# Attention scores and a filter product over 128 rows instead of 64, by zero padding, in a two-layer hybrid encoder

## The chip, the core and the metric

The kernel runs on one core of a Trainium2 chip. Such a core has a matrix engine (TensorE, PE in the profile; its weight loads are listed apart as PEld), two engines for elementwise work (VectorE, DVE; ScalarE, ACT), a slower general one (GpSimd, POOL), and SyncE (SP), which here only issues DMA transfers. Each engine works through its own instructions in program order, and semaphores hold one back until what it needs from another has been done.

The metric is device time of one execution in microseconds (us), smaller is better. Three executions of the kernel before took 1847.16, 1850.46 and 1852.89 us; the median is 1850.46 us.

## The reference

Two groups of tokens, a sample of 512 and a prompt of 256, go through the same two layers of width 1024. Each layer is a token mixer and a convolutional feed-forward network, with a norm ahead of and behind each. Layer 0 mixes with a gated MLP, layer 1 with two long convolutions whose filters a small MLP makes; beside the mixer, in both layers, runs cross-attention with 4 heads of 64 channels into 256 memory tokens of each group. Cut to what the change touches:

```python
def memory_cross_attention(q, mem, mem_g, w_kv):
    q = q.reshape(bsz, length, 4, 64)
    kv = (rms_norm(mem, mem_g) @ w_kv).reshape(bsz, 256, 2, 4, 64)
    k, v = kv[:, :, 0], kv[:, :, 1]
    s = jnp.einsum('bshd,bmhd->bhsm', q, k) * 64 ** -0.5     # the scores: 64 channels are summed
    p = jax.nn.softmax(s, axis=-1)
    return jnp.einsum('bhsm,bmhd->bshd', p, v).reshape(bsz, length, 256)

def hyena_filters(length, w1, b1, w2, b2, w3, freq):
    h = jnp.sin(fr * (feat @ w1 + b1))
    h = jnp.sin(fr * (h @ w2 + b2))                          # (length, 64)
    h = (h @ w3).reshape(length, 2, 2, 768)                  # 64 hidden units are summed
    return h * decay[:, None, None, :]

# per layer
att = memory_cross_attention(q, mem, ...)
x = x + rms_norm(concatenate([mix, att]) @ w_out)
x = x + rms_norm(conv_ffn(rms_norm(x)))
```

## The kernel before, in words

**Precision.** A float32 product is made of three matmuls in the type fp32r: each operand is split into a high part and the rest, and `mm3` (L497 to 501) adds high·high, high·low and low·high in one PSUM bank. The split is a pair of instructions, a copy to fp32r on ACT and a subtraction on DVE (`split`). So each weight tile that arrives by DMA (`wr`, 128x1024) becomes two tiles `ws`, and nearly all PE work is matmuls with 128 rows of weights and 256, 384 or 512 columns.

**Stages.** Layer 0: `pre` (norm and transposes), `kv0` (memory keys and values), the mixer, attention (`att0`), projection `out0`, then the feed-forward network (`up0`, `down0`). Layer 1 the same with `kv1`, `rows` and `conv` (short convolutions, and the long ones as matrix DFTs, tiles `dft` and `iv`), `att1`, `out1`, `up1`, `down1`. The filters for layer 1 are made during layer 0. In the profile the products of the feed-forward network and other projections are called `rp`, `fmp`, `fmb`, `fma`, `bQ`, `bP`, `bA`; `tps` are PE transposes through the tile `ident`.

**Keys.** `kv` (L819 to 866) makes, per layer, one tile `kT` [128, 2, 2, 512]: two heads on the upper and lower 64 partitions, then high and low part, head pair, and memory token. It is split from PSUM in 2 pieces of 128x512 per layer. The weights wk and wv go to buffers of their own (`own` true, tag `wkv`) or into the ring of ten `ws` buffers.

**Scores.** `attention` (L876 to 926) goes over 2 head pairs and 3 pairs of token tiles. For each, two PSUM banks `sc0`, `sc1` take the scores of the two heads: 2 token tiles × 3 products × 2 heads, the heads innermost, and each matmul uses the 64 partitions of its head (`r`) in both operands. That is 72 matmuls of 64 rows and 256 columns per layer. Behind them come the maximum (`mx`) on DVE, the exponentials (`e`) on ACT, transposes (`eps`) and `pv`.

**Filters.** `filters` (L1083 to 1163) makes `h` = `h2s`·`w3h` in 36 pairs: a matmul over 128 rows (the upper 64 the high part of the hidden units, the lower 64 their rest, against the high part of w3, which stands on both halves), and one over 64 rows for the low part of w3.

**Order of the work.** The program is recorded first. `Order` (L92 to 364) notes each operation with what it depends on, then `schedule` runs a list scheduler with its own costs (`cost`, L194 to 215): at each step the engine that can start earliest takes, among its ready operations, the one with the lowest rank, which is its number in the program plus a number from the table `BIAS` by stage and kind (L190: `pe`, `ve`, `dma`, `load`). None may be more than `AHEAD` operations beyond the oldest one not yet placed. All are emitted in that order from L364, so nearly every row of the profile has this line, and operations are told apart by tile names. Buffers come from small pools: 14 tiles of 8 KB per partition (`s8`), 27 of 4 KB (`s4`, of which 10 may be `ws`, 4 `wr`), and 8 PSUM banks.

Of the kernel before, what the change touches and what calls it, by code (L numbers as in the profile page):

```python
# [13 lines left out]
F32 = mybir.dt.float32  # L14
F32R = mybir.dt.float32r
I32 = mybir.dt.int32
AF = mybir.ActivationFunctionType
ALU = mybir.AluOpType
# [18 lines left out]
SEVEN = (1,)  # L37


AHEAD = 526  # L40
BIAS = {
    ('', 'dma'): -394,
    ('att0', 'pe'): -540, ('att0', 've'): -40,
    ('att1', 'pe'): -20, ('att1', 've'): -1151,
    ('block0', 'pe'): 175, ('block0', 've'): -278,
    ('block1', 'load'): 474, ('block1', 'pe'): -79, ('block1', 've'): -165,
    ('block2', 'load'): -843, ('block2', 'pe'): 33, ('block2', 've'): -155,
    ('conv', 'dma'): 395, ('conv', 'pe'): -273, ('conv', 've'): 32,
    ('down0', 'load'): -240, ('down0', 'pe'): -17,
    ('down0h0', 've'): -268,  # L50
    ('down0h1', 'dma'): -91, ('down0h1', 've'): 142,
    ('down1', 'load'): 163,
    ('down1h1', 'dma'): -343,
    ('filters', 'dma'): -120, ('filters', 'pe'): 253, ('filters', 've'): 275,
    ('gate', 'dma'): -215, ('gate', 've'): 147,
    ('kv0', 'dma'): -178, ('kv0', 'load'): -188, ('kv0', 'pe'): -894, ('kv0', 've'): -120,
    ('kv1', 'dma'): 162, ('kv1', 'load'): -202, ('kv1', 'pe'): -293, ('kv1', 've'): -427,
    ('mixed', 'pe'): -395, ('mixed', 've'): -1071,
    ('normv', 've'): -69,
    ('out0', 'load'): 518, ('out0', 'pe'): -124,  # L60
    ('out0h0', 've'): 79,
    ('out0h1', 'dma'): 302, ('out0h1', 'pe'): 31, ('out0h1', 've'): 102,
    ('out1', 'load'): -67, ('out1', 'pe'): -7,
    ('out1h0', 've'): 42,
    ('out1h1', 'dma'): -23, ('out1h1', 'pe'): 103, ('out1h1', 've'): -16,
    ('pre', 'dma'): -836, ('pre', 'load'): -835, ('pre', 'pe'): -114, ('pre', 've'): 48,
    ('presplit', 'dma'): -7, ('presplit', 've'): 464,
    ('q0', 'load'): -164, ('q0', 'pe'): 313, ('q0', 've'): 363,
    ('q1', 'load'): -618, ('q1', 've'): -315,
    ('rows', 'load'): -344, ('rows', 'pe'): 302, ('rows', 've'): -40,  # L70
    ('up0', 'load'): -444, ('up0', 'pe'): 22, ('up0', 've'): -873,
    ('up1', 'pe'): 59, ('up1', 've'): 343,
    ('x2', 'load'): 8, ('x2', 'pe'): 1,
}
LN_EPS = 1e-5
ATT_SCALE = 0.125
# [15 lines left out]
class Order:  # L92
# [100 lines left out]
    @staticmethod  # L193
    def cost(eng, method, kw, args, outs, ins):  # L194
        n = max(int(np.prod([c for s, c in x.ap[1:]])) for x in outs)
        psum = any(x.space == bass.MemoryType.PSUM for x in ins)
        if eng == "tensor":
            if method == "transpose":
                return 110
            if kw["rhs"].dtype == F32R:  # L200
                return 13.5 + n / 2.4 if n >= 256 else 229
            return 20 + 4 * n / 2.4
        if eng == "scalar":
            c = (52 if psum else 95) + 0.833 * n
            return c + (190 if isinstance(kw.get("bias"), bass.AP) or isinstance(kw.get("scale"), bass.AP) else 0) + \
                (90 if "accum_out" in kw else 0)
        if eng == "vector":
            if method in ("tensor_scalar", "tensor_copy") and not psum:
                return 68 + 0.522 * n
            if method == "tensor_reduce" or method == "bn_stats":  # L210
                n = max(int(np.prod([c for s, c in x.ap[1:]])) for x in ins)
            return (130 if method == "scalar_tensor_tensor" else 69) + 1.042 * n
        if eng == "gpsimd":
            return 180 + 2.105 * n
        return 450


# [209 lines left out]
class Prog:  # L427
# [391 lines left out]
    def kv(self, l, out, own):  # L819
        nc, a = self.nc, self.a  # L820
        g = self.gain(a["norm_mem"][l], name="gmem")
        kT = self.s8([128, 2, 2, 512], F32R, "kT")
        vS = self.s8([128, 2, 4, 256], F32R, "vS")
        out += [kT, vS]
        wk = wv = None
        for grp in range(2):
            mT = [self.s8([128, 8, 256], F32R, f"mT{h}") for h in range(2)]
            for i in range(2):
                m = self.t4(name="mem")
                nc.sync.dma_start(out=m, in_=a["mem"][2 * grp + i])  # L830
                mn = self.t4(name="mn")
                ss = self.small([128, 1], "mss")
                nc.scalar.activation(mn, m, AF.Square, accum_out=ss)
                r = self.rstd_of(ss, D, EPS, "mr")
                nc.vector.scalar_tensor_tensor(out=mn, in0=m, scalar=r, in1=g, op0=ALU.mult, op1=ALU.mult)
                s = slice(i * 128, (i + 1) * 128)
                for b in range(2):
                    ps = self.bank("mps")
                    for j in range(4):
                        k = 4 * b + j  # L840
                        nc.tensor.transpose(ps[:, j * 128:(j + 1) * 128], mn[:, k * 128:(k + 1) * 128], self.ident)
                    self.split(mT[0][:, 4 * b:4 * b + 4, s], mT[1][:, 4 * b:4 * b + 4, s],
                               ps.rearrange("p (k t) -> p k t", k=4))
                yield
            wk = wk or [self.wload(a["wk"][l, j], own) for j in range(2)]
            ps = self.bank("kps")
            for j in range(2):
                o = ps[:, j * 256:(j + 1) * 256]
                for k in range(KD):
                    ks = slice(k * 128, (k + 1) * 128)  # L850
                    self.mm3(o, wk[j][0][:, ks], wk[j][1][:, ks], mT[0][:, k], mT[1][:, k], k == 0, k == KD - 1)
            gs = slice(grp * 256, (grp + 1) * 256)
            self.split(kT[:, 0, :, gs], kT[:, 1, :, gs], ps.rearrange("p (j m) -> p j m", j=2))
            yield
            wv = wv or [self.wload(a["wv"][l, c], own) for c in range(2)]
            ps = self.bank("vps")
            for i in range(2):
                o = ps[:, i * 256:(i + 1) * 256]
                s = slice(i * 128, (i + 1) * 128)
                for k in range(KD):  # L860
                    w = wv[k // 4]
                    ks = slice((k % 4) * 256, (k % 4 + 1) * 256)
                    self.mm3(o, mT[0][:, k, s], mT[1][:, k, s], w[0][:, ks], w[1][:, ks], k == 0, k == KD - 1)
            self.split(vS[:, 0, 2 * grp:2 * grp + 2], vS[:, 1, 2 * grp:2 * grp + 2],
                       ps.rearrange("p (i m) -> p i m", i=2))
            yield
# [9 lines left out]
    def attention(self, q, kT, vS, put, hps=range(2)):  # L876
        nc = self.nc
        qS, qP = q
        for hp in hps:
            pS = [self.s8([128, 2, 2, NS], F32R, f"pS{h}") for h in range(2)]  # L880
            pP = [self.s4([128, 2, 2, NP], F32R, f"pP{h}") for h in range(2)]
            for ip in range(TT // 2):
                m0 = 0 if ip < 2 else 256
                qt, pt, o = (qS, pS, ip * 256) if ip < 2 else (qP, pP, 0)
                scs = [self.bank(f"sc{h}") for h in range(2)]
                for i in range(2):
                    t0 = o + i * 128
                    for n, (p, q) in enumerate(((0, 0), (0, 1), (1, 0))):
                        for h in range(2):
                            r = slice(h * 64, h * 64 + 64)  # L890
                            nc.tensor.matmul(scs[h][:, i * 256:(i + 1) * 256], lhsT=qt[r, p, hp, t0:t0 + 128],
                                             rhs=kT[r, q, hp, m0:m0 + 256], start=n == 0, stop=n == 2)
                for h in range(2):
                    sc = scs[h]
                    mx = self.small([128, 2], "mx")
# [187 lines left out]
    def filters(self):  # L1083
# [35 lines left out]
        for th in range(3):  # L1119
            for o in range(2):  # L1120
# [3 lines left out]
                self.tt(w3[:, 512:768], w3[:, 0:256], w3[:, 256:512], ALU.add)  # L1124
                self.tt(w3[:, 768:], w3[:, 0:256], w3[:, 256:512], ALU.subtract)
                wh = self.t4(shape=[128, 2, 512], dt=F32R, name="w3h")
                self.split(wh[:, 0], wh[:, 1], w3[:, 512:])
                hfS = [self.s8([128, 4, 2, 256], F32R, f"hfS{p}") for p in range(2)]
                hfP = [self.s4([128, 2, 2, 256], F32R, f"hfP{p}") for p in range(2)]
                for tp in range(3):  # L1130
# [5 lines left out]
                    for i in range(2):  # L1136
                        t = 2 * tp + i
                        ps = self.bank("h3")
                        s = slice(t * 128, (t + 1) * 128)
                        nc.tensor.matmul(ps, lhsT=hs[:, s], rhs=wh[:, 0], start=True, stop=False)  # L1140
                        nc.tensor.matmul(ps, lhsT=hs[:64, s], rhs=wh[:64, 1], start=False, stop=True)
                        for d in range(2):
                            self.tt(hf[:, i, d], ps[:, d * 256:(d + 1) * 256], dec[:, i * 256:(i + 1) * 256], ALU.mult)
                    if tp != 1:
# [71 lines left out]
    def mixer_b(self, hT, kvo):  # L1216
# [80 lines left out]
                            x2[j][:, t0:t0 + n].rearrange("p (i r) -> p r i", r=nr), ALU.mult)  # L1297
                    self.split(get(0, 2 * th + j), get(1, 2 * th + j), om[:, t0:t0 + n])

        kv = self.kv(1, kvo, True)  # L1300
        with nc.of("rows"):
            v = rows_of(0, 0)
        nc.run(kv, "kv1")
# [153 lines left out]
```

## Time and profile before

| | |
|---|---|
| median of 3 runs | 1850.46 us (1847.16 to 1852.89) |
| profiled execution, device time | 1850.47 us |
| its span in the trace | 1848.3 us |
| PE | 1802.5 us busy, 98% of the span, 9504 matmuls |
| DVE | 1142.6 us, 62% |
| ACT | 698.1 us, 38% |
| POOL | 73.3 us, 4% |
| mean granted clock of PE | 0.98 |

A row of the profile names the line, the engine, the operation, what it writes and reads (`out<-in`), the shape, and how often (x). For a matmul the first pair is rows × columns of the weights that it was loaded with, so `64*128` is a contraction over 64 partitions; the second is the moving operand. Matmul records overlap: each shows the time from its issue to its modelled end, and matmuls are pipelined, so what one costs is read from one start to the next, not from its length. In brackets behind a row stands how long the engine was idle before it, and what ended that. The slices of the page are 46.2 us wide; PEclk is the clock granted to PE in tenths.

### The profile page before, as it was taken

The page shows a single profiled execution, that of the slowest core. Times are in us where ns is not written, and L with a number is a line of the kernel's source. Part 1 is how long each engine was busy: PE and PEld are TensorE (multiplying, and loading weights), DVE is VectorE, ACT ScalarE, POOL GpSimd, SP SyncE. Part 2 cuts the span into 40 slices and gives each one's busy share as a digit, 9 for nine tenths or more (in the row PEclk, how much of TensorE's full clock was granted, in tenths as well). Part 3 has the DMA queues.
Part 4 walks back from the last instruction along what each step waited for, and adds up shares of the span by engine and source line. Part 5 has one row for each costly group of instructions (what it writes and reads, how often), then busy time and mean ns, then how long its engine had stood idle before and what let it go on. Part 6 is the DMA issues. An engine that isn't in the chain of part 4 may idle for free.

```text
span 1848.3 us, 23739 instructions
## 1 busy us (share of the span) xinstructions
PE 1802.5 (98%) x9504; PEld 1553.9 (84%) x9504; DVE 1142.6 (62%) x1671; ACT 698.1 (38%) x1073; POOL 73.3 (4%) x155
## 2 busy tenths in 40 slices
PE   8999999999999999999999999989699999999998
PEld 6978878788888888888898887868599999998886
DVE  6354465646455557553857894763888787874352
ACT  6363334323323326443521224142544344443330
POOL 1000020000000000000300000000300000000001
PEclk9999999999999999999999998979899999999999
DMA  6212162232233134588844232212322323356522
GB/s 259 81 40 80 35 211 84 65 110 78 79 115 103 59 124 163 201 295 301 316 159 160 82 95 98 69 56 70 126 86 86 114 87 103 103 201 249 189 79 102
DMA packets 66829, 236.18 MB, mean 128 GB/s; under 512 B 7475, under 2 KB 7679, under 8 KB 64160
## 3 DMA queue, kind: packets, MB, share of 16 engines
q1 hardware_dynamic: 66720, 234.68, 36.6%
q8 instruction: 75, 1.23, 0.3%
q14 instruction: 34, 0.28, 0.1%
HBM read 183.00 MB, written 51.64 MB: 127 GB/s over the span
## 4 chain that ended last, share of the span: by engine, by line
PE 88%; DVE 5%; issue 2%; ACT 1%; DMA 1%; POOL 1%; SPq 0%; DVEq 0%; ACTq 0%; POOLq 0%
PE rp L364 28%; PE fmp L364 11%; PE fmb L364 10%; PE fma L364 9%; PE bQ L364 7%; PE bP L364 5%; PE bA L364 5%; PE dft L364 3%; PE sc L364 2%; PE h L364 1%; PE iv L364 1%; PE kps L364 1%; PE pv L364 1%; PE vps L364 1%; DVE y L364 1%
## 5 line engine op out<-in xcount | busy, mean ns | idle before, releaser
L364 PE MATMUL fmp<-hTP,ws 128*128 128x256 f32 x1584 | 431.3, 296 | 0.0
L364 PEld LDWEIGHTS fmp<-hTP,ws 128*128 128x128 f32 x1584 | 295.5, 192 | 16.9 <-issue 11.5
L364 PE MATMUL fmb<-hTS,ws 128*128 128x512 f32 x792 | 295.8, 402 | 1.5 <-ACT ws L364 1.5
L364 PE MATMUL fma<-hTS,ws 128*128 128x512 f32 x792 | 291.4, 401 | 0.2 <-ACT ws L364 0.2
L364 PE MATMUL bQ<-x,ws 128*128 128x384 f32 x792 | 253.4, 335 | 0.0
L364 DVE TENSOR_TENSOR ws<-wr,ws 128x1024 fp32r<-128x1024 f32 (+1 forms) x188 | 214.8, 1157 | 56.8 <-PE rp L364 19.3
L364 ACT ACTIVATE ws<-wr 128x1024 fp32r<-128x1024 f32 (+1 forms) x188 | 186.0, 1005 | 148.9 <-PE rp L364 35.8
L364 PE MATMUL rp<-ws,xs 128*128 128x512 f32 x792 | 186.4, 390 | 0.0
L364 PEld LDWEIGHTS fmb<-hTS,ws 128*128 128x128 f32 x792 | 149.7, 189 | 38.7 <-issue 5.0
L364 PEld LDWEIGHTS fma<-hTS,ws 128*128 128x128 f32 x792 | 149.5, 189 | 33.7 <-ACT ws L364 0.7
L364 PE MATMUL bP<-x,ws 128*128 128x384 f32 x528 | 175.0, 334 | 0.0
L364 PEld LDWEIGHTS rp<-ws,xs 128*128 128x128 f32 x792 | 148.6, 188 | 30.9
L364 PE MATMUL bA<-x,ws 128*128 128x384 f32 x528 | 173.1, 336 | 0.0
L364 PEld LDWEIGHTS bQ<-x,ws 128*128 128x128 f32 x792 | 147.6, 188 | 0.2
L364 PE MATMUL rp<-ws,xsS 128*128 128x512 f32 x528 | 144.2, 390 | 0.0
L364 PEld LDWEIGHTS rp<-ws,xsS 128*128 128x128 f32 x528 | 99.0, 188 | 20.7
L364 PE MATMUL rp<-ws,mxS 128*128 128x512 f32 x384 | 108.0, 401 | 0.7 <-DVE ws L364 0.7
L364 PEld LDWEIGHTS bA<-x,ws 128*128 128x128 f32 x528 | 99.0, 188 | 0.5
L364 PEld LDWEIGHTS bP<-x,ws 128*128 128x128 f32 x528 | 99.0, 188 | 0.2
L364 PE MATMUL rp<-ws,hTS 128*128 128x512 f32 x288 | 89.3, 406 | 0.7 <-ACT hTS L364 0.7
L364 PEld LDWEIGHTS rp<-ws,mxS 128*128 128x128 f32 x384 | 71.5, 188 | 15.9 <-DVE ws L364 1.5
L364 PE MATMUL rp<-ws,xsP 128*128 128x512 f32 x264 | 82.4, 391 | 0.1
(259 smaller groups left out, 2661.5 us busy)
## 6 DMA issues: line engine op xcount, KB each, us to landing
wr<-w_up SPq DMA_DIRECT2D x88, 512.0 KB
wr<-w_down SPq DMA_DIRECT2D x44, 512.0 KB
wsp<-pw SPq DMA_DIRECT2D x20, 1024.0 KB
ws<-wsp SPq DMA_DIRECT2D x40, 512.0 KB
hc<-hsp SPq DMA_DIRECT2D x44, 384.0 KB
xs<-xr SPq DMA_DIRECT2D x18, 512.0 KB
praw<-bw SPq DMA_DIRECT2D x18, 512.0 KB
xr<-xs SPq DMA_DIRECT2D x18, 512.0 KB
```

What stands on the lines that cost most here:

```text
L364: getattr(getattr(self.real, eng), method)(*args, **kw)
```

## The change

Four things are changed.

1. `kT` becomes two tiles, one per head, each with all 128 partitions. The 64 partitions of the other head are set to zero by GpSimd (64x2048). The scores' matmuls use all 128 partitions of the queries and of that head's tile; the other head's queries meet zeros. The number of matmuls and their columns are the same. The two splits per layer become four on 64 partitions each.
2. In the filters, the low part of w3 has its lower 64 partitions set to zero by GpSimd (64x512, 6 times), and the second matmul of each pair uses 128 rows. The split is written out: ACT copies as before, DVE subtracts on 64 partitions.
3. The weights of the layer-1 keys and values no longer have buffers of their own; they go through the ring of `ws` tiles.
4. The planner has other numbers: `AHEAD`, the whole table `BIAS`, and the cost of a GpSimd operation.

```diff
-AHEAD = 526
+AHEAD = 427
 BIAS = {
-    ('att1', 'pe'): -20, ('att1', 've'): -1151,
+    ('att1', 'pe'): -14, ('att1', 've'): -1384,
...
         if eng == "gpsimd":
-            return 180 + 2.105 * n
+            return 300 + 1.1 * n if method == "memset" else 600
...
     def kv(self, l, out, own):
-        kT = self.s8([128, 2, 2, 512], F32R, "kT")
+        kT = [self.s8([128, 2, 2, 512], F32R, f"kT{h}") for h in range(2)]
+        for h in range(2):
+            nc.gpsimd.memset(kT[h][(1 - h) * 64:(2 - h) * 64].bitcast(F32), 0.0)
...
-            self.split(kT[:, 0, :, gs], kT[:, 1, :, gs], ps.rearrange("p (j m) -> p j m", j=2))
+            for h in range(2):
+                r = slice(h * 64, h * 64 + 64)
+                self.split(kT[h][r, 0, :, gs], kT[h][r, 1, :, gs], ps[r].rearrange("p (j m) -> p j m", j=2))
...
     def attention(self, q, kT, vS, put, hps=range(2)):
                         for h in range(2):
-                            r = slice(h * 64, h * 64 + 64)
-                            nc.tensor.matmul(scs[h][:, i * 256:(i + 1) * 256], lhsT=qt[r, p, hp, t0:t0 + 128],
-                                             rhs=kT[r, q, hp, m0:m0 + 256], start=n == 0, stop=n == 2)
+                            nc.tensor.matmul(scs[h][:, i * 256:(i + 1) * 256], lhsT=qt[:, p, hp, t0:t0 + 128],
+                                             rhs=kT[h][:, q, hp, m0:m0 + 256], start=n == 0, stop=n == 2)
...
     def filters(self):
-                self.split(wh[:, 0], wh[:, 1], w3[:, 512:])
+                nc.gpsimd.memset(wh[64:, 1].bitcast(F32), 0.0)
+                nc.scalar.activation(wh[:, 0], w3[:, 512:], AF.Copy)
+                self.tt(wh[:64, 1], w3[:64, 512:], wh[:64, 0].bitcast(F32), ALU.subtract)
...
-                        nc.tensor.matmul(ps, lhsT=hs[:64, s], rhs=wh[:64, 1], start=False, stop=True)
+                        nc.tensor.matmul(ps, lhsT=hs[:, s], rhs=wh[:, 1], start=False, stop=True)
...
-        kv = self.kv(1, kvo, True)
+        kv = self.kv(1, kvo, False)
```

The table moves instructions in the whole program. Three places matter for what follows.

PE, near the end of the layer-1 mixer, where the scores of the last head pair begin (`fmp` and `fmb` belong to the mixer's last projection, x2; `rp` to `out1`). Before:

```order
L364 MATMUL fmp<-hTP_1068,ws 128x256
L364 MATMUL sc_1600<-kT,qS 128x256
L364 MATMUL fmp<-hTP_1066,ws 128x256
L364 MATMUL sc_1601<-kT,qS 128x256
L364 MATMUL fmp<-hTP_1066,ws 128x256
L364 MATMUL sc_1600<-kT,qS 128x256
L364 MATMUL fmp<-hTP_1068,ws 128x256
L364 MATMUL sc_1601<-kT,qS 128x256
```

and with the change:

```order
L365 MATMUL eps<-ident,e 128x128
L365 MATMUL rp_1662<-ws,mxS_1363 128x512
L365 MATMUL sc_1620<-kT_1230,qS 128x256
L365 MATMUL rp_1662<-ws,mxS_1363 128x512
L365 MATMUL sc_1620<-kT_1230,qS 128x256
L365 MATMUL rp_1662<-ws,mxS_1364 128x512
L365 MATMUL sc_1621<-kT_1231,qS 128x256
L365 MATMUL sc_1620<-kT_1230,qS 128x256
L365 MATMUL sc_1621<-kT_1231,qS 128x256
```

The scores still stand one by one between other matmuls, but their neighbours are now matmuls of `out1`, so the end of the attention lies among the first products of the projection behind it.

GpSimd at the start of the program (`rstd` is the first norm's factor). Before:

```order
masks.py:197 MEMSET ident 128x128
L1335 MEMSET half 128x1
masks.py:199 ISA
masks.py:199 AFFINE_SELECT ident<-ident 128x128
L364 TENSOR_SCALAR rstdm<-ss 128x1
L364 TENSOR_TENSOR rstd<-rstdm,half 128x1
```

and with the change:

```order
masks.py:197 MEMSET ident 128x128
L1341 MEMSET half 128x1
L365 MEMSET kT_161 64x2048
masks.py:199 ISA
masks.py:199 AFFINE_SELECT ident<-ident 128x128
L365 MEMSET kT_162 64x2048
L365 TENSOR_SCALAR rstdm<-ss 128x1
L365 TENSOR_TENSOR rstd<-rstdm,half 128x1
```

Both memsets of layer 0 stand ahead of the first norm's factor, one of them ahead of `ident`.

ACT between `out1` and the feed-forward network of layer 1 (`x_…<-tps` takes transposes out of PSUM, `y,ss<-xr` is a norm's sum of squares, `ws<-wr` splits weights that are needed later). Before:

```order
L364 ACTIVATE x_1710<-tps 128x4x128
L364 ACTIVATE x_1716<-tps 128x4x128
L364 ACTIVATE ws<-wr 128x1024 x2
L364 ACTIVATE ws<-wt 128x1024
L364 ACTIVATE ws<-wr 128x1024
L364 ACTIVATE y,ss<-xr 128x1024 x2
```

and with the change:

```order
L365 ACTIVATE x_1722<-tps 128x4x128
L365 ACTIVATE x_1710<-tps 128x4x128
L365 ACTIVATE y,ss<-xr 128x1024
L365 ACTIVATE x_1714<-tps 128x4x128
L365 ACTIVATE ws<-wt 128x1024
L365 ACTIVATE ws<-wr 128x1024
```

The norm's sum of squares no longer stands behind four splits of weights.

More of the change, by code (lines that the diff above doesn't have):

```diff
@@ L37 @@
 SEVEN = (1,)
-AHEAD = 526
+AHEAD = 427
 BIAS = {
-    ('', 'dma'): -394,
-    ('att0', 'pe'): -540, ('att0', 've'): -40,
-    ('att1', 'pe'): -20, ('att1', 've'): -1151,
[L45 to L73, printed above, removed]
@@ new lines @@
+    ('', 'dma'): -2,
+    ('att0', 'pe'): -316, ('att0', 've'): -260,
+    ('att1', 'pe'): -14, ('att1', 've'): -1384,
+    ('block0', 'pe'): -163, ('block0', 've'): -39,
+    ('block1', 'load'): 340, ('block1', 'pe'): -167, ('block1', 've'): 145,
+    ('block2', 'load'): 1617, ('block2', 've'): -9,
+    ('conv', 'dma'): 560, ('conv', 'pe'): -564, ('conv', 've'): -528,
+    ('down0', 'load'): 958, ('down0', 'pe'): 163,
+    ('down0h0', 've'): -4337,
+    ('down0h1', 'dma'): 2296, ('down0h1', 'pe'): 305, ('down0h1', 've'): -207,
@@ new lines @@
+    ('down1', 'load'): 1243, ('down1', 'pe'): -12,
+    ('down1h0', 've'): 261,
+    ('down1h1', 'dma'): 293, ('down1h1', 've'): -320,
+    ('filters', 'dma'): 790, ('filters', 'pe'): 146, ('filters', 've'): 1331,
+    ('gate', 'dma'): 137, ('gate', 'pe'): -8, ('gate', 've'): 289,
+    ('kv0', 'dma'): -214, ('kv0', 'load'): 897, ('kv0', 'pe'): -937,
+    ('kv1', 'dma'): -395, ('kv1', 'load'): -76, ('kv1', 'pe'): -858, ('kv1', 've'): 21,
+    ('mixed', 'pe'): -486, ('mixed', 've'): 124,
+    ('normv', 've'): -1344,
@@ new lines @@
+    ('out0', 'load'): 532, ('out0', 'pe'): -124,
+    ('out0h0', 've'): -1398,
+    ('out0h1', 'dma'): 1199, ('out0h1', 'pe'): 67, ('out0h1', 've'): -313,
+    ('out1', 'load'): 13, ('out1', 'pe'): -143,
+    ('out1h0', 've'): 816,
+    ('out1h1', 'dma'): -336, ('out1h1', 'pe'): -113, ('out1h1', 've'): -391,
+    ('pre', 'dma'): -1178, ('pre', 'load'): -660, ('pre', 'pe'): -165,
+    ('presplit', 'dma'): -820, ('presplit', 've'): -839,
+    ('q0', 'pe'): 232, ('q0', 've'): -564,
+    ('q1', 'load'): 1748, ('q1', 'pe'): 140, ('q1', 've'): 123,
@@ L74 @@
+    ('rows', 'load'): -821, ('rows', 'pe'): 293, ('rows', 've'): 294,
+    ('up0', 'pe'): -154, ('up0', 've'): -1419,
+    ('up1', 'dma'): -300, ('up1', 'load'): 324, ('up1', 'pe'): 61, ('up1', 've'): -419,
+    ('x2', 'load'): -53, ('x2', 'pe'): -34, ('x2', 've'): 159,
 }
```

## The prediction

> **What bounds the kernel now.** I read the page first, its busy shares and chain, then PE's waits, then single stretches of the timeline.
>
> ```profile
> span 1848.3 us, 23739 instructions
> PE 1802.5 (98%) x9504; PEld 1553.9 (84%) x9504; DVE 1142.6 (62%) x1671; ACT 698.1 (38%) x1073; POOL 73.3 (4%) x155
> PEclk9999999999999999999999998979899999999999
> PE 88%; DVE 5%; issue 2%; ACT 1%; DMA 1%; POOL 1%; SPq 0%; DVEq 0%; ACTq 0%; POOLq 0%
> ```
>
> PE is the bound: 98% busy, 88% of the chain. Time can only be won where PE is shown busy and does little, or waits. The clock row has one weak place, slices 25 to 29 (1109 to 1340 us). Busy is no measure of work here, since a record lasts until its modelled end; what counts is the distance between starts. The waits of the weight loads name the tiles this change touches ("issue": held by nothing that the profile shows):
>
> ```profile
> PEld sc L364 <- issue: 11.8, 49, 0.4
> PEld fmp L364 <- issue: 11.5, 47, 0.8
> PEld h L364 <- issue: 10.7, 36, 0.4
> ```
>
> (us in total, times, longest.) All 36 narrow loads of `h` are among them. The timeline around one shows how:
>
> ```profile
> 355.36 0.28 PE L364 MATMUL fmp<-hTP,ws 128*128 128x256 f32 x1
> 355.47 0.40 PE L364 MATMUL fmb<-hTS,ws 128*128 128x512 f32 x1
> 355.71 0.28 PE L364 MATMUL fmp<-hTP,ws 128*128 128x256 f32 x1
> 355.91 0.18 PEld L364 LDWEIGHTS h<-w3h,h2s 64*128 64x128 f32 x1 [0.25 <-issue]
> 355.92 0.49 PE L364 MATMUL h<-w3h,h2s 64*128 64x512 f32 x1
> 356.34 0.19 PEld L364 LDWEIGHTS fmp<-hTP,ws 128*128 128x128 f32 x1 [0.24 <-issue]
> 356.34 0.38 PE L364 MATMUL fmp<-hTP,ws 128*128 128x256 f32 x1
> ```
>
> Start to start, a 256-column matmul of 128 rows takes 0.11 to 0.12 us (355.36 to 355.47) and one of 512 takes 0.24 (to 355.71). The one before the 64-row `h` takes 0.21 instead of 0.11, and `h` itself 0.42 instead of 0.24: the 64-row load starts only 0.01 us before its matmul, not beside the matmul ahead, and the same on the way back. A change of row form costs about 0.28 us in and out, whatever it computes.
>
> For the scores there are two cases, crowded and alone:
>
> ```profile
> 87.33 1.77 PE L364 MATMUL sc<-kT,qS 64*128 64x256 f32 x24
> 89.03 0.50 PE L364 MATMUL fmb<-hTS,ws 128*128 128x512 f32 x1
> ...
> 110.27 0.50 PE L364 MATMUL pv<-pS,vS 128*128 128x512 f32 x1
> 110.70 0.38 PE L364 MATMUL sc<-kT,qS 64*128 64x256 f32 x1
> 111.01 0.49 PE L364 MATMUL rp<-ws,hTS 128*128 128x512 f32 x1
> ```
>
> Twenty-four in a row take 1.70 us, 0.071 each: the two heads' matmuls, on different halves of the rows, run beside one another. Alone, `pv` takes 0.43 instead of 0.24 and `sc` 0.31 instead of 0.12: 0.38 lost.
>
> Layer 1 is the worst. There scores alternate one by one with `fmp`:
>
> ```profile
> 1191.82 0.38 PE L364 MATMUL sc<-kT,qS 64*128 64x256 f32 x1
> 1192.13 0.39 PE L364 MATMUL fmp<-hTP,ws 128*128 128x256 f32 x1
> 1192.44 0.38 PE L364 MATMUL sc<-kT,qS 64*128 64x256 f32 x1
> ```
>
> A pair takes 0.62 us instead of 0.24. In such stretches the clock falls as well:
>
> ```profile
> core 0: us, PE busy (x) PEld busy (x) DVE busy (x) ACT busy (x) POOL busy (x), PEclk, DMA share, GB/s
> 1108.30:1123.00 14.70, 14.70 (x43) 9.70 (x42) 1.92 (x6) 4.71 (x13) 0.00 (x0) 0.66 0.48 174
> 1113.00:1123.00 10.00, 10.00 (x27) 6.94 (x27) 1.92 (x6) 4.71 (x13) 0.00 (x0) 0.50 0.25 102
> 1134.00:1141.00 7.00, 7.00 (x38) 4.36 (x37) 5.81 (x15) 4.75 (x14) 0.00 (x0) 1.00 0.27 77
> 1191.60:1219.90 28.30, 28.30 (x66) 16.48 (x64) 9.23 (x14) 3.87 (x8) 0.00 (x0) 0.56 0.06 19
> 1195.00:1219.90 24.90, 24.90 (x55) 14.60 (x54) 5.99 (x11) 2.97 (x7) 0.00 (x0) 0.50 0.07 21
> 1219.90:1245.00 25.10, 20.18 (x112) 16.84 (x112) 24.25 (x51) 17.18 (x46) 0.00 (x0) 0.82 0.27 84
> ```
>
> Granted clock 0.50 from 1113 to 1123 and from 1195 on, with PE issuing a matmul every 0.31 to 0.45 us and never idle for longer. I read the half clock as a result of the alternation: in a pair PE streams columns for 0.24 of 0.62 us, and looks half idle to whatever grants the clock.
>
> [...]
>
> **The change part by part.** The sum starts from the profiled execution, 1850.47 us (2.2 us outside its span), which is also the median.
>
> *Filters:* 36 × 0.28 = **−10.1**. The columns are unchanged.
>
> *Scores, layer 0:*
>
> ```profile
> L364 PEld LDWEIGHTS sc<-kT,qS x15: 182/183/183, 102.0 to 116.9; 64*128 64x128 f32 x15
> ...
> 132.14 1.33 PE L364 MATMUL sc<-kT,qP 64*128 64x256 f32 x17
> 133.40 0.49 PE L364 MATMUL pv<-pS,vS 128*128 128x512 f32 x1
> ```
>
> Fifteen stand alone: 15 × 0.38 = −5.7. Where they are crowded padding loses: 24 × 0.12 = 2.9 for 1.7, and 17 × 0.12 = 2.0 for 1.3, together +1.9. The other 16 stand in small groups where entry and loss about cancel. **−3.8.**
>
> [...]
>
> *Scores, layer 1:* three stretches, each against what its matmuls would take at 0.12 and 0.24:
>
> ```profile
> L364 PE MATMUL fmb<-hTS,ws 128*128 128x512 f32 x3 | 2.0, 683 | 0.0
> ...
> L364 PE MATMUL fmb<-hTS,ws 128*128 128x512 f32 x1 | 0.4, 392 | 0.0
> ```
>
> (The only wide matmuls of the first and the third.) First: 40 × 0.12 + 3 × 0.24 = 5.5 for 14.7, **−9.2**. Second, 1134 to 1141: at best 38 × 0.12 = 4.6 for 7.0; some are fp32 transforms, which take longer, so **−1.9**. Third: 65 × 0.12 + 0.24 = 8.0 for 28.3, **−20.3**. This holds if no other limit appears in the shortened stretches. Over the first, DMA is 48% busy, so no transfer is shown to hold it. That the new order places the scores elsewhere changes nothing in the sum as long as a 128-row matmul costs 0.12 anywhere.
>
> *Behind them.* Two PE waits stand on attention's tail and the convolution:
>
> ```profile
> 1221.91 0.80 PE L364 MATMUL iv<-dfti,A 128*128 128x128 f32 x2 [1.68 <-ACT e L364]
> 1224.69 5.64 PE L364 MATMUL iv<-dfti,A 128*128 128x128 f32 x30 [1.98 <-DVE zP L364]
> ...
> PE tps L364 <- DVE y L364: 19.6, 8, 9.5
> 1325.46 2.01 ACT L364 ACTIVATE ws<-wr 128x1024 fp32r<-128x1024 f32 x2
> ```
>
> From 1219.9 to 1245 DVE is busy 24.25 of 25.1 us, so this stretch gains little unless other PE work covers DVE's. In the new order matmuls of `out1` stand among the last scores; they are that cover. Gain between 0 and 6 (3.7 of waits, and half clock on the first 30 `iv`): **−3**. If the cover is missing, DVE is late next, for `mx` and the splits of the exponentials.
>
> At the step from `out1` to the feed-forward network PE waits for `y`, 9.5 us the longest time. ACT's splits of weights, 2 × 2.0 us (two of four last 2.01), no longer stand ahead of the squares: between 0 and −8, I take **−4**, one row of four splits.
>
> *Start.* Two memsets of 2048 elements on POOL ahead of the first `rstd`, one ahead of `ident`. No row shows one so long:
>
> ```profile
> L1335 POOL MEMSET half<- 128x1 f32 x1 | 0.1, 99 | 0.0
> masks.py:197 POOL MEMSET ident<- 128x128 f32 x1 | 0.2, 204 | 0.3 <-POOLq L1447 0.3
> masks.py:199 POOL TENSOR_SCALAR_AFFINE_SELECT ident<-ident 128x128 f32<-128x128 f32 x1 | 0.3, 292 | 0.0
> ...
> 5.88 0.19 POOL L364 TENSOR_SCALAR rstdm<-ss 128x1 f32<-128x1 f32 x1 [4.60 <-ACT hn L364]
> ```
>
> By the slope of the memsets, (204 − 99) / 127 = 0.83 ns an element, each takes 1.8 us: 3.6 us, inside POOL's 4.60 us of idle time. By the select's whole rate, 2.28 ns, each takes 4.7 and the pair ends 4.8 us late, with the norm, its transposes and the first `rp` behind it. It is a memset, so the first is nearer; SP also sends two input tiles ahead of the first weights: **+1** (0 to +4.8).
>
> *The rest.* Splits of keys on half the partitions:
>
> ```profile
> L364 ACT ACTIVATE kT<-kps x4: 597/598/599, 61.7 to 951.7; 128x512 fp32r<-128x512 f32 x4
> ```
>
> four more on ACT (0.60 each) and on DVE, beside PE, at engines that are 38% and 62% busy: 0. The later memsets are on POOL, 4% busy: 0. Layer 1's key weights in the ring of `ws` take buffers from the weights of the next stage: 0 to +4, **+1**.
>
> Sum: −10.1 − 3.8 − 9.2 − 1.9 − 20.3 − 3 − 4 + 1 + 1 = −50.3. Forecast **1800 us**.
>
> **The rivals.** *Part of the late gain is given back* (0.15). From 1191.6 to 1245 DVE has 9.2 + 24.3 = 33.5 us of work; PE's would shrink to 8.0 and some 17. If `out1` covers nothing, DVE sets the end and 8.5 us return; add the 7 hoped for behind them, and the time is 1815. For it: those 24.25 of 25.1 us. Against it: the new order.
>
> *The half clock has another cause and stays* (0.08). Then a padded pair takes 0.48 and not 0.24: the third stretch 55 × 0.12 = 6.6 more, the first 27 × 0.12 = 3.2 more, 1810. For it: full clock in the second stretch, which has scores too. Against: the other two are those with the strict alternation.
>
> *It goes further* (0.06): the waits for `y`, 19.6 us, are halved by the new order: 1790 or less, about 1785. For it the chain's 5% of DVE; against it that `y` needs the last product in any case.
>
> *Slower: the gap is not the row form's* (0.05). If a lone load of scores waits for something else that padding leaves (its tile in another buffer, its bank), all drains stay, and the side-by-side of the heads is lost: at least the 41 crowded ones at 0.05 each, +2, and where the new order sets them apart 41 × 0.31 = +13; with 1 + 1 for start and ring, 1854 to 1865, say 1859. It decides once lone scores still cost over 0.3 us more than their 0.12. For it: only loads are seen waiting, and "issue" names no cause. Against: `h` and `sc` share nothing but 64 rows, and `fmp` waits just the same on the way back.
>
> **How the numbers follow.** Forecast 0.66, its own range 1790 to 1812. With the first two rivals above and the third below, 8 in 10 lie between 1783 and 1820. Faster by over 0.3% (5.5 us, about what a measurement of this kernel can tell from no change): 0.94, the first four cases less 0.01. Slower: 0.04 of the last rival's 0.05. Within 0.3%: those two hundredths.
>
> **What would show it.** No waits of `sc` and `h` loads on "issue"; all 72 matmuls of `h` in one form with a mean near 0.39; scores of 128 rows at 0.12 from start to start; clock 1.00 from 1108 to 1230. Wrong would be: half clock where scores alternate, PE waits on DVE at the end of layer 1's attention, or a first `rp` later than before by over 2 us.

## The result, and the profile after

The changed kernel takes **1784.62 us** (median; 1784.29 to 1785.99 in 4 runs) against 1851.31 us before (1847.16 to 1852.89, 4 runs): a ratio of 0.9645, 95% interval 0.9627 to 0.9662, or about 66 us less. The forecast was 1800 us with a range of 1783 to 1820. The direction and most of the places were right. The gain is 16 us larger than the likeliest case: the time lies below the 1790 to 1812 that the prediction gave to its own account, and inside the wide range by 1.6 us.

The page of the profile after, the lines that answer to those shown of before:

```profile
span 1782.5 us, 23756 instructions
PE 1745.7 (98%) x9504; PEld 1542.9 (87%) x9504; DVE 1143.0 (64%) x1675; ACT 696.3 (39%) x1075; POOL 82.2 (5%) x165
PEclk9999999999999999999999999999799999999999
PE 93%; DVE 5%; DMA 1%; issue 1%; ACT 1%; POOL 1%; POOLq 0%; SPq 0%; DVEq 0%; ACTq 0%
```

PE has the same 9504 matmuls and is still 98% busy, in 66 us less. Of the three weak slices of the clock one is left, the step from `out1` to the feed-forward network (slice 29, 1248 to 1292 us).

The waits of PE's weight loads after, the three largest kinds that "issue" ended (the others come to 0.5 us or less each):

```profile
PEld tps L365 <- issue: 5.8, 5, 4.3
PEld fmp L365 <- issue: 1.1, 2, 0.8
PEld vtp L365 <- issue: 0.6, 2, 0.4
```

`sc` and `h` are no longer among them, and `fmp` has 1.1 us instead of 11.5. By tiles, `h` has one form, at the duration that the wide half had before:

```profile
L365 PE MATMUL h<-w3h,h2s x72: 391/398/403, 353.5 to 653.9; 128*128 128x512 f32 x72
```

Scores among the matmuls of `out1`, in the timeline after:

```profile
1175.90 0.28 PE L365 MATMUL sc<-kT,qS 128*128 128x256 f32 x1
1176.01 0.39 PE L365 MATMUL rp<-ws,mxP 128*128 128x512 f32 x1
1176.24 0.28 PE L365 MATMUL sc<-kT,qS 128*128 128x256 f32 x1
1176.36 1.09 PE L365 MATMUL rp<-ws,mxP 128*128 128x512 f32 x4
```

A lone score now takes 0.11 us from start to start and its neighbour 0.23. Windows of the profile after (columns as before: us, busy time and count by engine, clock, DMA share, GB/s):

```profile
1075.00:1090.00 15.00, 15.00 (x89) 13.46 (x88) 11.96 (x23) 4.83 (x10) 0.00 (x0) 1.00 0.48 161
1148.80:1202.00 53.20, 52.85 (x307) 45.05 (x307) 38.89 (x69) 24.09 (x57) 0.00 (x0) 1.00 0.24 80
1236.00:1272.00 36.00, 22.13 (x106) 18.30 (x105) 33.69 (x48) 18.83 (x37) 12.20 (x25) 0.75 0.43 155
```

From the first scores of layer 1 through the end of its attention the clock is 1.00 and PE waits for almost nothing. At the last row's step it still waits, as before.

**Where the time went.** To compare two orders of the same matmuls I gave each matmul the time that it takes undisturbed, from start to start in these traces (0.11 us for 128 columns, 0.11 to 0.12 for 256, 0.17 for 384, 0.23 for 512), added these up along PE's order (some 1700 us in all in both kernels), and read at which time of the trace each kernel has done the same amount. The differences to before, in us, are worked out from the starts in the traces; "form alone" is the first experiment below. Where the orders differ, a row moves by up to 2 us if the short matmuls are priced otherwise.

```
PE work done   what lies there                     forecast   form alone   the change
0 to 50        start, keys of layer 0               +1           0.0         +0.7
50 to 200      mixer and attention, layer 0         -3.8        -4.9         -4.9
200 to 300     out0 to the feed-forward network      0          -1.0         -5.4
300 to 650     feed-forward, with the filters      -10.1       -14.8        -15.2
650 to 1000    to the end of kv1                    +1          -0.2         -0.8
1000 to 1100   att1, first two stretches           -11.1       -11.1        -10.5
1100 to 1150   att1, third stretch and tail        -23.3       -19.5        -27.8
1150 to 1200   out1 to the feed-forward network     -4          +0.7         -3.0
1200 to end                                          0          +0.7         +0.5
sum                                                -50.3       -50.1        -66.4
```

(The spans differ by 65.8 us: behind PE's last matmul the change has 0.6 us more.)

### The profile page after: what moved, and what is told of

Same layout as the page of the kernel before. It is cut to its first block, busy times and chain, and to the rows that moved or that the text cites. A ratio compares the mean times of both kernels' runs of the same rounds, so it can differ in the third digit from the quotient of the medians.

```text
span 1782.5 us, 23756 instructions
## 1 busy us (share of the span) xinstructions
PE 1745.7 (98%) x9504; PEld 1542.9 (87%) x9504; DVE 1143.0 (64%) x1675; ACT 696.3 (39%) x1075; POOL 82.2 (5%) x165
## 4 chain that ended last, share of the span: by engine, by line
PE 93%; DVE 5%; DMA 1%; issue 1%; ACT 1%; POOL 1%; POOLq 0%; SPq 0%; DVEq 0%; ACTq 0%
PE rp L365 32%; PE fmp L365 10%; PE fma L365 10%; PE fmb L365 10%; PE bQ L365 8%; PE bA L365 5%; PE bP L365 5%; PE dft L365 3%; PE iv L365 1%; PE kps L365 1%; PE vps L365 1%; PE tps L365 1%; PE h L365 1%; PE sc L365 1%; PE pv L365 1%; DVE x L365 1%
## 5 line engine op out<-in xcount | busy, mean ns | idle before, releaser
L365 PE MATMUL fmp<-hTP,ws 128*128 128x256 f32 x1584 | 405.4, 286 | 0.0
L365 DVE TENSOR_TENSOR ws<-wr,ws 128x1024 fp32r<-128x1024 f32 (+1 forms) x192 | 219.7, 1158 | 118.0 <-ACT ws L365 79.6
L365 PEld LDWEIGHTS fmp<-hTP,ws 128*128 128x128 f32 x1584 | 288.4, 190 | 3.1 <-issue 1.1
L365 PE MATMUL fmb<-hTS,ws 128*128 128x512 f32 x792 | 290.9, 399 | 0.0
L365 PE MATMUL bQ<-x,ws 128*128 128x384 f32 x792 | 247.6, 334 | 0.0
L365 PE MATMUL rp<-ws,xsS 128*128 128x512 f32 x528 | 136.9, 390 | 0.0
L365 PE MATMUL rp<-ws,mxS 128*128 128x512 f32 x384 | 117.2, 406 | 0.2 <-DVE ws L365 0.2
L365 PE MATMUL rp<-ws,hTS 128*128 128x512 f32 x288 | 83.8, 403 | 0.0
L365 DVE TENSOR_TENSOR xs<-hc,xs 128x1536 fp32r<-128x1536 f32 x22 | 38.6, 1758 | 64.6 <-ACT ws L365 36.6
```

What stands on the lines that cost most here:

```text
L365: getattr(getattr(self.real, eng), method)(*args, **kw)
```

## The experiments

Theory: a short run of 64-row matmuls among 128-row ones costs PE time at entry and exit (by the prediction's readings 0.28 us for `h` and 0.38 for a lone score; called a drain below), and layer 1's half clock follows from that. Against it: the gain belongs to the new order of work; the half clock has another cause; 64 rows are slow wherever they stand. All ratios are to the kernel before, with its runs on the same chip.

**1. The form alone.** The order of before stays the same on every engine, and only the operands are widened. Without zeros a score sums both heads, so this shows PE's time under padding with none of its overhead (a lone score takes 0.12 us from start to start in experiment 2, 0.11 in the change).

```diff
-    lhsT=qt[r, p, hp, t0:t0 + 128], rhs=kT[r, q, hp, m0:m0 + 256]
+    lhsT=qt[:, p, hp, t0:t0 + 128], rhs=kT[:, q, hp, m0:m0 + 256]
-    lhsT=hs[:64, s], rhs=wh[:64, 1]
+    lhsT=hs[:, s], rhs=wh[:, 1]
```

> The kernel before, with its own order of instructions unchanged on every engine; only the operands of the scores' and of the filters' second matmuls are widened from 64 to 128 rows, with no zeros, no memsets and no further buffers (so each score sums both heads of a pair, and the filters add a small product: a part of the computation is changed). Theory (the row form costs a drain on each entry and exit, and half clock follows from it): -10.1 for the filters, -3.8 and -31.4 for the scores, 0 to -6 behind them: 1799 to 1806 us, granted clock 1.00 from 1108 to where the last scores end. If the 16 us that the change won beyond the forecast also come from the form: about 1786. Rival (the gain is the new order's): 1850. Rival (the half clock has another cause): about 1815, clock 0.50 in the same two stretches.

Measured: 1801.82 us against 1850.02, ratio 0.9737 (0.9723 to 0.9752), 48 us less. So nearly three quarters of the gain is the form's, at an unchanged order, and the other 17 us are not. What form does not mend is the tail of layer 1's attention:

```profile
1170.38 0.49 PE L364 MATMUL iv<-dfti,A 128*128 128x128 f32 x2 [1.84 <-ACT e L364]
1173.16 5.89 PE L364 MATMUL iv<-dfti,A 128*128 128x128 f32 x30 [2.29 <-DVE zP L364]
```

and, from the same kernel's windows, the clock falls with them:

```profile
1168.00:1180.00 12.00, 7.79 (x45) 7.18 (x43) 11.94 (x29) 6.02 (x20) 0.00 (x0) 0.72 0.31 89
```

DVE is busy for 11.94 of 12 us: the bound that the first rival named. With the order unchanged the two waits even grow, from 3.7 to 4.1 us. The matmuls that took the 53.4 us from 1191.6 to 1245 before take 33.9 here, and DVE is busy for 33.0 of them.

**2 and 3. Scores alone, filters alone.** The first and the second half of that edit.

> As the run before, but only the scores are widened, order unchanged. Theory: 1809 to 1816 us, clock 1.00 in the stretches of layer 1's scores; the loads of scores no longer wait. Rival (half clock has another cause): 1825, with the drains gone and clock 0.50 still there. Rival (gap is not the form's): 1852 to 1863, lone scores still 0.31 from start to start.

Measured: 1814.97, ratio 0.9808 (0.9793 to 0.9823), inside the theory's interval. The timeline of the stretch that took 28.3 us before:

```profile
1176.72 0.27 PE L364 MATMUL fmp<-hTP,ws 128*128 128x256 f32 x1
1176.84 0.28 PE L364 MATMUL sc<-kT,qS 128*128 128x256 f32 x1
1176.95 0.28 PE L364 MATMUL fmp<-hTP,ws 128*128 128x256 f32 x1
...
1183.43 0.28 PE L364 MATMUL fmp<-hTP,ws 128*128 128x256 f32 x1
1183.55 0.40 PE L364 MATMUL sc<-kT,qP 128*128 128x256 f32 x2
1184.58 0.97 PE L364 MATMUL sc<-kT,qP 128*128 128x256 f32 x6 [0.63 <-ACT e L364]
```

The same alternation of the same matmuls, each 0.12 us after the other: 6.7 us up to 1183.55, with the last eight scores some 8.6, of which 0.63 wait for ACT's exponentials. The granted clock over it, in the windows of this run, is 1.00:

```profile
1170.50:1179.00 8.50, 8.50 (x55) 7.74 (x54) 8.37 (x10) 1.97 (x3) 0.00 (x0) 1.00 0.72 222
1179.00:1187.00 8.00, 5.92 (x48) 5.51 (x46) 8.00 (x17) 4.46 (x12) 0.00 (x0) 1.00 0.21 65
```

> Only the filters' second matmul is widened to 128 rows, order unchanged. Theory: 36 x 0.28 = 10.1 us less, 1840 us. The changed kernel won 16.6 us over the stretch of the filters (matched by PE work done); if all of that is the form's: 1834. Rival (gap is not the form's): 1850.

(Here too the widened matmul adds the small product that was named for experiment 1.)

Measured: 1837.37, ratio 0.993 (0.9915 to 0.9945), 12.7 us less, between the two sizes. By PE work done, 14.5 us are won by the end of the filters, 0.40 for each of the 36, and about 1 comes back at `kv1`. The forecast had 0.28 each. The row that it left out, from before's timeline, behind the rows shown in the prediction:

```profile
356.34 0.38 PE L364 MATMUL fmp<-hTP,ws 128*128 128x256 f32 x1
356.56 0.40 PE L364 MATMUL fmb<-hTS,ws 128*128 128x512 f32 x1
```

The matmul behind the 64-row one takes 0.22 instead of 0.11 as well: its own load starts only with it, at 356.34, and the load of the next at 356.44, 0.12 us ahead of that matmul. Entry 0.10, `h` itself 0.18, the one behind 0.11: 0.39.

**4. Grouped, with 64 rows.** The kernel before, with PE's order changed in one respect: the twelve scores of a pair of banks stand side by side.

```diff
     def emit(self):
         order = self.schedule()
+        order = self.group(order)
```

(`group` itself is left out here. It moves the matmuls of `sc0` and `sc1` of one step to a place where the operands of all are ready. In the trace the 144 scores stand in 13 runs: one of 24, eight of 12, four of 6.)

> The kernel before with 64 rows everywhere; the only edit is PE's order: the twelve score matmuls of a pair of banks (6 and 6 in three cases) stand side by side, where most stood alone. Theory (what costs is the number of entries and exits): some 59 lone entries become 13, a group of 12 takes about 12 x 0.071 + 0.3 = 1.15 us; layer 1's three stretches fall as with padding, clock 1.00: 1808 to 1816 us. Rival (64 rows are slow wherever they stand): no gain, 1850.

Measured: 1814.94, ratio 0.9807 (0.979 to 0.9823): with 64 rows the same gain as from widening the scores. From its timeline:

```profile
1104.79 0.98 PE L390 MATMUL sc<-kT,qS 64*128 64x256 f32 x12
1105.69 1.59 PE L390 MATMUL fmp<-hTP,ws 128*128 128x256 f32 x11
```

Twelve in 0.90 us, and in layer 1 the clock stays at 1.00 until 1187.01, behind the last scores. So 64 rows are not slow when the two heads stand side by side; entering and leaving is. This is the plainest result of the study: what was paid for was the interleaving.

**5. The new order with 64 rows.** The changed kernel, its order and its zeros untouched, operands cut back.

```diff
-    lhsT=qt[:, p, hp, t0:t0 + 128], rhs=kT[h][:, q, hp, m0:m0 + 256]
+    lhsT=qt[h * 64:h * 64 + 64, p, hp, t0:t0 + 128], rhs=kT[h][h * 64:h * 64 + 64, q, hp, m0:m0 + 256]
-    lhsT=hs[:, s], rhs=wh[:, 1]
+    lhsT=hs[:64, s], rhs=wh[:64, 1]
```

> The changed kernel with its order unchanged on every engine, zeroed tiles and memsets kept, but scores and the filters' second matmul over 64 rows again. Its order has more lone scores than the one before (about 90 of 144). Theory: 36 x 0.28 = +10.1 and at least 90 x 0.38 = +34 less what the crowded ones win back (about 2), so 1826 us at full clock, up to 1850 and more where the clock falls to 0.50 among them. Rival (the new order won the time, the form nothing): 1785 to 1790.

Measured: 1830.39, ratio 0.9886 (0.9871 to 0.99). Undoing the form costs 46 us, near the lower end of what was expected. The parts were not as expected: 72 scores stand alone, not 90, and the clock does fall. It is 0.50 for 6.8 us from 107.88, behind scores that mostly alternate with transposes, and for 10.2 us from 1193.32, where they alternate with 256-column `fmp`. Where layer 1's scores stand among the 512-column `rp` it holds:

```profile
1194.00:1200.00 6.00, 6.00 (x13) 3.54 (x14) 1.12 (x2) 1.06 (x1) 0.00 (x0) 0.50 0.50 170
1212.00:1218.00 6.00, 6.00 (x20) 3.10 (x20) 3.00 (x6) 2.51 (x4) 0.00 (x0) 1.00 0.28 87
```

The four corners:

```
                 64 rows    128 rows
order before     1850       1801.8
order after      1830.4     1784.6
```

Form is worth 48 and 46 us, the order 20 and 17: nearly independent of one another. (The runs stood on different chips; by the ratios it is 49 and 45, 21 and 17. "Order after" holds everything else of the change as well: the zeros, their memsets, the split keys and the ring for the key weights.)

**6. The new order, filters padded, scores with 64 rows in groups.** A candidate for something better than both.

> The changed kernel with the filters padded, but scores over 64 rows again and the matmuls of a pair of banks put side by side in PE's order (groups of 6 to 24). Theory: a group of 12 takes 12 x 0.071 + 0.3 = 1.15 us against 12 x 0.12 = 1.44 padded; twelve such groups win 3.5 us at most, so 1781 to 1785, about the same or a little better than the change. Rival (any 64-row matmul among others brings the clock down): 1800 or more.

Measured: 1785.68, ratio 0.9644 (0.963 to 0.9659), the same as the change. The 3.5 us that side-by-side running might have won did not show; by PE work done 1.8 are won in layer 0, and 1.2 of them are given back in layer 1's attention.

**7 and 8. The table and the operations apart.** Both paddings with the old table; the old operations with the new table.

> All of the change but the planner's numbers: both paddings, the ring for layer 1's key weights, and the table, the bound and the costs of before. The planner lays the order out anew since the operations are not the same, so its order is neither of the two. Theory (form is worth about 50, the table the rest): 1795 to 1810 us. If the table is worth nothing: 1785. If the old numbers fit the new operations badly, with waits at the steps between stages: 1815 or more.

> The kernel before with the new table and bound alone, 64 rows and no padding. Theory: the lone scores cost what they did or more, since the table was not made for these operations: 1840 to 1870 us, with clock 0.50 where scores stand alone in layer 1. Rival (the table won the time): about 1800.

Measured: 1819.29, ratio 0.9827 (0.9812 to 0.9842), and 1851.86, ratio 1.0002 (0.9989 to 1.0015). The first met neither the theory's interval nor its nearest rival, only the third case: the old numbers, with the numbering of operations shifted by the new ones, make an order with some 4 us lost at the start, some 3 at `kv1`, and 9 to 10 less won at layer 1's attention than with the order of before. The second is worth nothing in sum: by PE work done it wins some 4.5 us at `out0` and some 4 in layer 1's attention, and loses some 10 in layer 0's. As I read it, such a table fits the operations that it was made for, and the order's 17 to 20 us belong to the pair.

**9 to 12. What brings the clock down.** Two and four make the half clock a consequence of the alternation: the clock was 1.00 over the stretch that had 0.56 before. My idea was that the clock follows the share of time in which PE streams columns. If so, more work in the alternating stretch should make it faster. Nine issues each score of the last head pair twice (and halves the softmax factor), ten is its control at 128 rows, eleven issues the neighbours twice, twelve issues every fourth neighbour five times.

```diff
                 eng, method, args, kw = self.ops[i][:4]
+                if i in self.twice:
+                    getattr(getattr(self.real, eng), method)(*args, **dict(kw, stop=False))
+                    kw = dict(kw, start=False)
```

(The lines of nine and ten; `twice` holds the 36 scores of layer 1's last head pair. In eleven it holds the 29 `fmp` ahead of a lone score, in twelve every fourth of these, with the repeat in a loop of four.)

> The kernel before (64 rows, old order), with more work: each of the 36 score matmuls of the last head pair of layer 1 is issued twice in a row into the same bank, and the factor in the softmax is halved. A lone score and its neighbour then stream 3 x 0.12 us of columns in about 0.74 us (49%) instead of 2 x 0.12 in 0.62 (39%); in the changed order with 64 rows, scores next to 512-column matmuls, at 49% too, kept clock 1.00. Theory (clock falls with the streamed share): 28 x 0.74 + 16 x 0.071 + 0.2 = 22 us for the stretch from 1191.6 instead of 28.3, clock 1.00, and about 2 behind it: about 1842 us, faster although 36 matmuls are added. Rival (the clock falls by the alternation of row forms or by another cause): 28 x 1.26 = 35 us and more, clock 0.50: about 1858.

> The same doubled scores with all scores widened to 128 rows (each score sums both heads of a pair: a part of the computation is changed), order unchanged. Full clock either way, so the doubling only adds 36 x 0.12 = 4.3 us to the run with widened scores: 1819 us.

> The kernel before (64 rows, old order) with more work of the other kind: the 29 matmuls over 128 rows that stand right ahead of a lone score of the last head pair of layer 1 are issued twice in a row (so some products of x2 count double: a part of the computation is changed). A lone score now comes every 0.74 us, just as when the scores were doubled, but of the 0.36 us streamed only 0.12 is over half the rows: counted by rows, (0.24 + 0.06) / 0.74 = 41% against 32% there, 29% in the kernel before, and 41% in the changed order with 64 rows, where the clock held. Theory (what counts is the streamed share weighted by rows): clock 1.00, 22 us for the stretch from 1191.6 instead of 28.3, about 1842 us although 29 matmuls are added. Rival (the strict alternation of row forms brings the clock down, whatever is streamed): clock 0.50 again, 28 x 1.26 = 35 us, about 1856.

> Nearly the same work added as with the doubled neighbours (28 repeated 256-column matmuls over 128 rows instead of 29), the same 41% of rows streamed on average, but the repeats stand together: after every fourth lone score of the last head pair of layer 1 its neighbour is issued five times in a row, so the alternation is broken every 2.5 us by about 0.5 us of plain matmuls. (Some products of x2 count five times: a part of the computation is changed.) With doubled neighbours the clock fell after 8 us of unbroken alternation, with doubled scores after 4.7, in the kernel before after 3.3; in the changed order with 64 rows it held where stretches of alternation of at most 3 us were broken by plain matmuls. Theory (an unbroken stretch of alternation brings the clock down): clock 1.00, 28 x 0.62 + 28 x 0.12 + 1.2 = 22 us from 1191.6, total about 1842 us. Rival (the average streamed share over some 8 us decides): it falls as with doubled neighbours, 1855 us.

Measured: nine 1855.69 (ratio 1.0036, 1.0019 to 1.0052); ten 1818.14 (ratio 0.9834), as expected, 3.2 us more than experiment 2 (4.8 by the ratios); eleven 1855.39 (1.004, 1.0023 to 1.0056); twelve 1857.96 (1.003, 1.0014 to 1.0046). The idea, at the shares that I had put on it, fell three times: the clock was 0.50 in each. But not at the same point. Windows of eleven:

```profile
1196.00:1200.00 4.00, 4.00 (x18) 2.64 (x17) 1.19 (x2) 1.73 (x2) 0.00 (x0) 1.00 0.37 125
1200.00:1204.00 4.00, 4.00 (x15) 2.53 (x14) 1.46 (x3) 0.00 (x0) 0.00 (x0) 0.78 0.02 6
1204.00:1208.00 4.00, 4.00 (x11) 2.43 (x11) 0.44 (x1) 0.00 (x0) 0.00 (x0) 0.50 0.01 2
```

and of nine:

```profile
1192.00:1196.00 4.00, 4.00 (x17) 2.60 (x17) 1.39 (x2) 1.76 (x2) 0.00 (x0) 0.97 0.38 116
1196.00:1200.00 4.00, 4.00 (x11) 2.52 (x10) 0.06 (x1) 0.00 (x0) 0.00 (x0) 0.50 0.04 15
```

Eleven alternates from 1194.25 and holds for 8.0 us; nine, which begins at 1190.38, falls after 5.4, at 1195.79. What lies behind it is in the last section: my shares were counted too high, and the changes of the clock lie on a grid of 3.41 us.

## Why the prediction was right, and where it was not

**The bound and the drains: right.** PE's waits on "issue" for `sc` and `h` are gone and those for `fmp` fell from 11.5 us to 1.1, lone scores take 0.11 to 0.12, and experiments 1 to 3 win it at an unchanged order. The last rival (the gap is not the form's, 1859) is out. That it is the interleaving, not the 64 rows, experiment 4 shows; the prediction had read this from the run of 24. One reading was off: at half clock the starts in the alternation stand 0.51 us apart (1197.00, 1197.51 and so on), not 0.45 at most; that was the mean of a stretch that ends with eight scores side by side.

**Filters: a mis-sized term.** −10.1 stood for what is −14 to −15 by the stretch (12.7 in the medians of experiment 3). The step that failed is "a change of row form costs about 0.28 us in and out": two starts were counted and the third, of the matmul behind, was not. It was one row further down.

**Scores: right.** Layer 0 −4.9 for −3.8; layer 1's first two stretches −11.1 at unchanged order for −11.1; the third −19.5 for −20.3.

**The half clock is a result of the alternation: right.** The second rival (it has another cause and stays, 1810) is out by experiments 2 and 4, where the same stretch ran at 1.00.

**Behind them: right in place, too small in size.** The tail's −3 rested on `out1` covering it. At the unchanged order nothing is won there, and the first rival's mechanism holds: it had 33.5 us of DVE's work set the length of scores and tail, and 33.9 it is. Its price was too high. Of 53.4 us the sum left 30.1, so DVE's 33.5 give back 3.4 and not 8.5; the 25 that it set beside them counted more of the tail as won than the forecast did. In the changed kernel the cover is complete, PE busy for 52.85 of 53.2 us, and the two kernels differ by 8.3 us there. The upper end of 6 was too low: it counted the two waits and the first `iv`. In experiment 1 the tail held 4.1 us of those waits, up to some 2.4 of lost clock (0.50 from 1171.17 to 1178.00, of which PE waits for 2.0), and shorter gaps beside them. The step from `out1` to the network: −3.0 for −4; PE's waits there for `y` fell from 16.4 us to 12.6:

```profile
PE tps L364 <- DVE y L364: 16.4, 4, 9.5
PE tps L365 <- DVE y L365: 12.6, 3, 8.0
```

The third rival gave the total (1785) and not the reason: it had the waits for `y` halved, 19.6 us in the whole kernel, and they fell to 14.6. That the time lies inside the stated range is in part luck: the extra gain came from the filters' third start (5), from the tail (4.5) and from a step that had no term.

**Not seen at all:** the step from `out0` to layer 0's network, 5.4 us better in the change, 1.0 in the form alone. Before, PE's sixteen transposes of `y` came in one piece behind a wait of 2.38 us at 273.16, and PE waited 1.54 us for weights behind them; the clock was 0.50 in two windows, from 273.27 and from 280.09. After, eight come in one piece behind a wait of 1.97 us, others stand among the first `fma`, and one such window is left, from 267.49. I had read the moved instructions at three places and not there. That these 4.4 us, the 8.3 of the tail and the 3.7 of `out1` come from the new order follows from comparing with experiment 1. Two of the three follow the table in the other runs too: by the same count the step at `out0` is 4 to 6 us shorter in every run with the new table (5, 6 and 8) and at most 1.1 in those with the old (1 to 4 and 7), the one at `out1` 2 to 3.5 against none. None was undone by itself.

**Start: right.** The rows of POOL after, from its timeline:

```profile
1.02 1.80 POOL L365 MEMSET kT<- 64x2048 f32 x1
2.90 0.29 POOL masks.py:199 TENSOR_SCALAR_AFFINE_SELECT ident<-ident 128x128 f32<-128x128 f32 x1
3.15 1.80 POOL L365 MEMSET kT<- 64x2048 f32 x1
5.76 0.19 POOL L365 TENSOR_SCALAR rstdm<-ss 128x1 f32<-128x1 f32 x1 [0.82 <-ACT hn L365]
```

The slope of the small memsets gave 1.8 us and 1.80 it is; the factor of the norm waits for ACT, not for POOL. The first `rp` does start 2.2 us later than before (12.92 for 10.73), a sign that I had named as one of an error. It was a bad sign to name: by then PE has done sixteen transposes instead of eight, and the delay by work done is 0.7 us. The ring for layer 1's weights: nothing lost that can be seen (−0.8 for +1); it was not undone by itself either.

## What to carry to other kernels

Look for short matmuls of another row form among full ones, and count the starts around one until they are even again: the matmul ahead, itself, and the one behind (0.10, 0.18 and 0.11 us for `h`). Either pad them or put them side by side; for the scores of this kernel both won the same (1814.97 and 1814.94 us), and a group of twelve in two heads was fast with no zeros (0.90 us). When a stretch on the matrix engine gets shorter, ask which engine had its work covered by it: here the saving of the last stretch was whole only with an order that put other matmuls over the tail (27.8 us by PE work done, 19.5 at the order of before).

## What the runs showed of the hardware

**The changes of the clock lie on a grid.** A trace records each stretch of granted clock with its start, its length and its share. In the 14 profiles of this study each change lies on a grid of 3.41 us, to within a hundredth of a step, with another phase in each run. In the kernel before the clock fell at 1112.95, rose at 1123.19, fell at 1194.87 and rose at 1229.00: distances of 3, 21 and 10 steps. The shortest stretches at 0.50, two in the kernel before (from 273.27 and 280.09) and one in the changed one (from 267.49), last 3.413 us, one step. A step of this grid is called a window below.

**No idle gap stands ahead of the fall at 1194.87.** PE issued a matmul every 0.31 us in the window ahead of it. So I counted, for each window at full clock, how much of it PE streamed columns times the share of rows in use, and whether half clock came next. A matmul of 384 columns takes 173 ns from start to start and one of 512 takes 227 (medians in the kernel before), so I estimate a column at 0.42 ns (0.108 us for 256), laid from the matmul's start. In the kernel before this gives 0.25 for the window ahead of 1112.95 and 0.31 for the one ahead of 1194.87. Over all 14 profiles:

```
streamed share, by rows     half clock next   full clock next
under 0.20                        48                 1
0.20 to 0.34                      31                18
0.34 to 0.38                       6                22
over 0.38                          0               all
```

The plain fp32 transforms, which take 0.215 us for 256 columns, count here like the others; at their own time the second row is 32 and 10, the third 7 and 7. Counted by columns without the rows, windows fall up to a share of 0.45 and hold from 0.19, so rows narrow the overlap but do not end it. Experiments 9, 11 and 12 fit: the windows ahead of the fall had 0.28, 0.36 and 0.36. They do not prove it, since one window of eleven at 0.36 had held. My 32% and 41% were too high, since I had used 0.12 us for what counts 0.108 here. An alternation is not needed either: windows of 128-row matmuls alone, with waits in them, fell at shares of 0.25 to 0.36 too. What the clock follows stays open; no run here separates rows from anything that goes with them, and between 0.19 and 0.38 the count does not decide.
